# Where split weights stand in SBUF: from two pools on 512-byte boundaries to one ring whose blocks are offset for 256-column products

## The chip, the core and the metric

One core of one Trainium2 chip runs the whole kernel. The time is that of one execution on the device in microseconds, a median over runs. "The kernel before" is the version that the profile below was taken of, "after" the version with the change.

## What is computed

Two layers of an encoder trunk on 512 tokens of width 1024, in float32. Layer 0 mixes the tokens with retention and neighbourhood attention, layer 1 with a bidirectional SSD (Mamba-2) mixer. Each layer ends in the same channel mixer, which is where most of the changed products are:

```python
def conv_geglu_ffn(hn, w_up, conv_w, conv_b, w_down):
    u = depthwise_conv_centered(hn @ w_up, conv_w, conv_b)
    gate, val = jnp.split(u, 2, axis=-1)
    return (jax.nn.gelu(gate, approximate=True) * val) @ w_down

for layer in range(DEPTH):                      # DEPTH = 2
    hn = rms_norm(x, norm_mix_pre[layer])
    m = retention_na_mixer(hn, ...) if layer % 2 == 0 else ssd_mixer(hn, ...)
    x = x + rms_norm(m, norm_mix_post[layer])
    f = conv_geglu_ffn(rms_norm(x, norm_ffn_pre[layer]), ...)
    x = x + rms_norm(f, norm_ffn_post[layer])
```

w_up is 1024 x 5632 (22 tiles of 128 columns for the gate, 22 for the value), w_down 2816 x 1024.

## The kernel before

**Split operands.** TensorE multiplies in a float32 form of shorter mantissa (float32r). To keep float32 accuracy each operand is split into a high and a low part: ScalarE casts the source into the high part (L107), VectorE subtracts that from the source into the low part (L108). A product then takes three instructions, `mm3` (L114): high x high (L116), low x high (L117), high x low (L118). In projections to feature-major tiles the weights are the stationary operand, loaded into the array in blocks of 128 x 128 (128 partitions, 128 values of 4 bytes, so 512 bytes a partition), and the activations `xh`, `xl` stream through as 256 or 512 columns. In the profile PE is the stream of a product and PEld the load of its stationary block; the load of the next block runs while the present product streams.

**Weights on their way.** A weight unit is 128 x 1024 values. SyncE's queue loads it into one of three `wst` buffers; the split writes it into a buffer of the pool `whi` and one of `wlo`, four deep each (L41-42):

```python
hi, lo = self.whi.tile([P, 1024], R32, name="whi"), self.wlo.tile([P, 1024], R32, name="wlo")
with self.tc.high_priority(60):
    self.split(hi, lo, st, behind, low_behind)
```

This stands in `wunit` (L89), in `down_strassen` (L298), in `up_strassen` (L443) and, with 512 columns, in the step-size projection of the SSD mixer (L940). Each buffer starts on a multiple of 512 bytes, so every 128-column block does, too. In the step-size projection a block has only 64 columns, so every second one starts 256 bytes behind a boundary.

**Products with 256 columns.** Most products stream 512 columns. Three places stream 256:

- `up_strassen` (L429) computes two tiles each of gate and value as seven products of quarter matrices instead of eight. A call issues 7 x 2 x 4 `mm3`, 168 products, into `mm` and `pu` tiles. It is called at f = 6, 10, 14 and 18 (`UP`) of each FFN: eight calls. Its weights are sums of loaded units, made on VectorE ahead of the split. Its activations come from `combos` (L391), whose operands `xR`, `xS` go into tiles of the tags b1h, b1l, s3, e2.
- Each FFN starts with its first two tiles of gate and value in two halves of the tokens, since the second half is normalised later. The two units for the second tile are split into tiles that are free then, of the tags b1h, b1l and e2 (`extra`).
- The SSD mixer starts its first three tiles in halves likewise (L1224).

**The order of work.** A tile scheduler places the instructions of each engine by priorities from the order of the program; it may move those that aren't bound by data. Between engines semaphores hold the order. After the two halves the FFN goes tile by tile (f = 2 to 21), a tile being two units of 24 products of 512 columns, then a convolution on ScalarE (L507) and VectorE (L508, L509), gelu (L514) and the product of gate and value (L516). A down projection of seven quarter products with 512 columns (`down_strassen`) ends it. The SSD mixer (`mixer1`, L900) interleaves projections with the scan by hand-written lists of steps.

Of the kernel before, what the change touches and what calls it, by code (L numbers as in the profile page):

```python
# [8 lines left out]
F32 = mybir.dt.float32  # L9
R32 = mybir.dt.float32r  # L10
BF16 = mybir.dt.bfloat16
# [6 lines left out]
P = 128  # L18
S = 512
NT = S // P  # L20
D = 1024
# [4 lines left out]
HK = NF // 2  # L26
HW = S // 2
QUARTER = HK * P * S


class Env:


    def __init__(self, ctx, tc):
        self.tc, self.nc = tc, tc.nc
        nc = self.nc
        pool = lambda name, bufs, **kw: ctx.enter_context(tc.tile_pool(name=name, bufs=bufs, **kw))
        self.const = pool("const", 1)
        self.res = pool("res", 1)
        self.wst = pool("wst", 3)  # L40
        self.whi = pool("whi", 4)  # L41
        self.wlo = pool("wlo", 4)
        self.gain = pool("gain", 2)
        self.tmp = pool("tmp", 7)
        self.small = pool("small", 6)
        pool("pad", 1).tile([P, 48], F32, name="pad")
        self.mm = pool("mm", 4, space=PSUM)
        self.px = pool("px", 4, space=PSUM)
        self.dram = pool("dram", 1, space=DRAM)


        head = self.const.tile([P, 96 + P], F32, name="head")
        self.ident, self.mhalf = head[:, 96:], head[:, 0:1]
        make_identity(nc, self.ident)
        nc.vector.memset(self.mhalf, -0.5)

        xe = self.res.tile([P, NT, D + 32], F32, name="x")
        nc.vector.memset(xe[:, :, D:D + 1], (EPS * D) ** 0.5)
        self.x, self.xe = xe[:, :, :D], xe[:, :, :D + 1]
        self.junk = self.const.tile([P, 1280], BF16, name="junk")  # L60
        self.operands()
        self.late, self.xs, self.turned, self.chores = [], {}, {}, []

    def operands(self):
# [13 lines left out]
            self.together([m], [behind])  # L78
        return st

    def wunit(self, src, parts=None, st=None, behind=None, low_behind=None):

        if st is None:
            st = self.wload(src)
        halves = slice(0, 512), slice(512, 1024)
        if parts is None:
            hi, lo = self.whi.tile([P, 1024], R32, name="whi"), self.wlo.tile([P, 1024], R32, name="wlo")  # L89
            with self.tc.high_priority(60):  # L90
                self.split(hi, lo, st, behind, low_behind)
            return [(hi[:, c], lo[:, c]) for c in halves]
        with nullcontext() if behind else self.tc.high_priority(60):
            for j, c in enumerate(halves):
                self.split(parts[j], parts[j + 2], st[:, c], behind)
        return [(parts[j], parts[j + 2]) for j in range(2)]
# [181 lines left out]
def down_strassen(E, big, pool, w, ts, H, first, g_post, done):  # L278
# [15 lines left out]
    def weights(i, u, extra=None):  # L294
        cols = 1024 if u < HK // 2 else 512
        st = stage(i, u, cols)
        if extra is None:
            hi, lo = E.whi.tile([P, 1024], R32, name="whi"), E.wlo.tile([P, 1024], R32, name="wlo")  # L298
        else:
            hi, lo = extra[:, :1024], extra[:, 1024:]  # L300
        with tc.high_priority(150):
            E.split(hi[:, :cols], lo[:, :cols], st)
        return [(hi[:, c:c + 512], lo[:, c:c + 512]) for c in range(0, cols, 512)]
# [31 lines left out]
    st = {}  # L335
# [93 lines left out]
def up_strassen(E, w_up, f, X, G, V):  # L429
# [10 lines left out]
        return st  # L440

    def parts(st):
        hi, lo = E.whi.tile([P, 1024], R32, name="whi"), E.wlo.tile([P, 1024], R32, name="wlo")  # L443
        E.split(hi, lo, st)
        return hi, lo

# [49 lines left out]
def ffn(E, w_up, cw, w_down, ts, g_post_row, done, w1=None):  # L496
# [3 lines left out]
    with ExitStack() as ctx:  # L500
# [15 lines left out]
            nc.vector.tensor_tensor(H[:, f], g, v, op=ALU.mult)  # L516

        def extra(tags):
            t = [hp.tile([P, 2048 // len(tags)], R32, name="x" + n, tag=n) for n in tags]
            t = t if len(t) == 2 else [t[0][:, :1024], t[0][:, 1024:]]  # L520
            return [x[:, c:c + 512] for x in t for c in (0, 512)]

        u0, u1, st = w1 or (E.wunit(w_up[0, 0]), E.wunit(w_up[1, 0]), None)

        behind = E.turned[1][1] if w1 else None
        w0 = [[u0, u1], [E.wunit(w_up[0, 1], extra(("b1h", "b1l")), st, behind=behind),
                         E.wunit(w_up[1, 1], extra(("e2",)), behind=behind)]]
        cwt = cp.tile([P, 2, NF, 4], F32, name="cwt")
        nc.sync.dma_start(cwt, cw)
        cwn = cp.tile([P, NF, 3], F32, name="cwn")  # L530
# [369 lines left out]
def mixer1(E, w_dt, w_fm, cw, dtc, cols, mask, w_out, g_post_row, done, ahead):  # L900
# [8 lines left out]
    with ExitStack() as ctx:  # L909
# [1 line left out]
        one, two, four = pool("m1", 1), pool("m1b", 2), pool("m1d", 4)  # L911

        few = pool("m1s", 1)
        few.tile([P, 32], F32, name="gap")
        few.tile([P, 32], F32, name="pad")

        cwt = few.tile([P, NG, 6, 6], F32, name="cwt")
        nc.sync.dma_start(cwt, cw)
        um = one.tile([P, P], F32, name="um")
# [16 lines left out]
        def steps():  # L936

            st = E.wst.tile([P, 512], F32, name="wst")
            nc.sync.dma_start(st, w_dt)
            wh = E.whi.tile([P, 512], R32, name="whi")  # L940
            wl = E.wlo.tile([P, 512], R32, name="wlo")
            E.split(wh, wl, st)
            ps = E.mm.tile([P, S], F32, name="mm")
            for k in range(KD):
# [276 lines left out]
                project(o, i)  # L1221
            silus(o)

        w0 = [E.wunit(w_fm[0, i]) for i in range(3)]  # L1224
        p0 = [E.mm.tile([P, S], F32, name="mm") for _ in range(3)]
        for c in range(2):
            for i, (w, ps) in enumerate(zip(w0, p0)):
# [57 lines left out]
def trunk(tc, x, norms, ab, ssd, ffns, out):  # L1285

    nc = tc.nc
    with ExitStack() as ctx:
        E = Env(ctx, tc)
        w0 = []  # L1290
        for t in range(NT):
            nc.sync.dma_start(E.x[:, t, :], x[t * P:(t + 1) * P])
            if t == 0:
                g0 = E.bcast(norms[0, 0])

                nc.scalar.activation(E.junk[:, :1], E.mhalf, AF.Square)
            else:
                w0.append(E.wunit(ab[0][0, len(w0)]))
        for t in range(NT):
            E.norm(t, g0)  # L1300
            last = E.turn(t, 0 if t else 100)
            if t == 0:

                junk = E.px.tile([P, P], F32, name="idle", tag="px")
                E.together([nc.tensor.transpose(junk, E.ident, E.ident) for _ in range(6)], [last])

        def then(row):
            g = []

            def done(t):  # L1310
                if not g:
                    g.append(E.bcast(row))
                E.norm(t, g[0])
            return done

        def store(t):
            E.xs.pop(t, None)
            for h in range(2):
                c = slice(h * 512, h * 512 + 512)
                nc.sync.dma_start(out[t * P:(t + 1) * P, c], E.x[:, t, c])  # L1320

        ts = [E.dram.tile([4, QUARTER], F32, name=f"ts{i}") for i in range(2)]
        mixer0(E, w0, *ab, norms[0, 1], then(norms[0, 2]))
        E.chores = sums(E, ffns[0][2], ts[0])
        ffn(E, *ffns[0], ts[0], norms[0, 3], then(norms[1, 0]))
        w1 = []

        def ahead(w):
            up = ffns[1][0]
            w1.extend((E.wunit(up[0, 0]), E.wunit(up[1, 0], low_behind=w), E.wload(up[0, 1])))  # L1330

        mixer1(E, *ssd, norms[1, 1], then(norms[1, 2]), ahead)
        E.chores = sums(E, ffns[1][2], ts[1])
        ffn(E, *ffns[1], ts[1], norms[1, 3], store, w1)
        while E.late:
            E.flush()
# [119 lines left out]
```

## Time and profile before

| | us |
|---|---|
| median of three runs | 1370.33 (1370.28 to 1371.69) |
| the profiled execution | 1372.97 |
| its span, first to last instruction | 1371.2 |
| TensorE busy (PE) | 1344.3 |
| VectorE busy | 1088.5 |
| ScalarE busy | 815.2 |
| 24 products of 256 columns, by a stage's 20.15 for 168 | 2.88 |
| 24 products of 512 columns, by 80.00 for 353 | 5.44 |

A row of a group gives line, engine, operation, out <- in, count, busy time and the mean of one. A row of the timeline gives start and duration in us first. Products overlap: each lasts longer (0.28 us with 256 columns) than it is from its start to the next one's start (0.12 us), so the pace is read from starts or from counts in a stretch, not from durations. In the rows by stretches the columns are: the stretch, its length, then busy time and count of PE, PEld, VectorE, ScalarE and GpSimd, the granted share of the clock, the share of the DMA engines, and GB/s.

### The profile page before, as it was taken

The numbers are of one execution on the slowest core, as the hardware profiler recorded it, in microseconds if no ns is written. First come the engines' busy times: TensorE is split into PE (matmuls) and PEld (weight loads), VectorE is DVE, ScalarE is ACT, GpSimd is POOL, SyncE is SP. The second block draws the span as 40 slices with busy tenths as digits, with TensorE's granted clock in tenths as the row PEclk, the third lists the DMA queues.
The fourth block names the chain that finished last, engine by engine and source line by source line (L and its number), as shares of the span: only waits on it lengthen the run. The fifth ranks groups of instructions, "written<-read, shape, count | busy, mean of one in ns | idle before, by whom it ended". The sixth has DMA issues, their size and how long they took to land.

```text
span 1371.2 us, 19491 instructions
## 1 busy us (share of the span) xinstructions
PE 1344.3 (98%) x7352; PEld 1136.2 (83%) x7352; DVE 1088.5 (79%) x1524; ACT 815.2 (59%) x1345; POOL 111.5 (8%) x130
## 2 busy tenths in 40 slices
PE   7999999999999999999999999999999999999997
PEld 6877777798999888888778788787878899998886
DVE  7368878696768889697878876898789877888876
ACT  5356667453554566664878778477555455556563
POOL 1001110100111100020000110000010001110000
PEclk9999999999999999999999999999999999999999
DMA  7443232126779946654566455174433678994654
GB/s 298 144 138 99 89 100 93 49 93 218 256 210 233 250 147 193 197 201 128 142 180 194 119 178 179 48 204 110 147 128 127 224 249 214 234 242 131 196 179 145
DMA packets 73471, 229.90 MB, mean 168 GB/s; under 512 B 8352, under 2 KB 9120, under 8 KB 72864
## 3 DMA queue, kind: packets, MB, share of 16 engines
q1 hardware_dynamic: 58320, 167.30, 37.3%
q0 software_dynamic: 7168, 46.14, 13.4%
q10 hardware_dynamic: 7888, 15.21, 4.1%
q8 instruction: 58, 0.95, 0.3%
q14 instruction: 37, 0.30, 0.1%
HBM read 221.01 MB, written 51.64 MB: 199 GB/s over the span
## 4 chain that ended last, share of the span: by engine, by line
PE 83%; ACT 6%; DVE 5%; DMA 3%; issue 2%; POOL 1%; DVEq 0%; SPq 0%; POOLq 0%; ACTq 0%
PE mm L116 23%; PE mm L118 23%; PE mm L117 23%; PE pu L118 2%; PE pu L117 2%; PE pu L116 2%; PE pi L1122 1%; PE st L1071 1%; ACT pb L1101 1%; DMA pb<-pd 1%; PE py L1142 1%; ACT whi L107 1%; DVE wlo L108 1%; DMA wst<-in_c_fm 1%; PE pt L173 1%
## 5 line engine op out<-in xcount | busy, mean ns | idle before, releaser
L116 PE MATMUL mm<-xh,whi 128*128 128x512 f32 (+1 forms) x1024 | 382.5, 374 | 0.8 <-ACT z L1041 0.4
L118 PE MATMUL mm<-xl,whi 128*128 128x512 f32 (+1 forms) x1024 | 381.6, 373 | 1.0 <-DVE xl L108 0.5
L117 PE MATMUL mm<-xh,wlo 128*128 128x512 f32 (+1 forms) x1024 | 381.3, 373 | 1.0 <-DVE wlo L108 1.0
L108 DVE TENSOR_TENSOR wlo<-wst,whi 128x1024 fp32r<-128x1024 f32 (+1 forms) x232 | 280.9, 1216 | 89.9 <-ACT whi L107 88.3
L107 ACT CAST whi<-wst 128x1024 fp32r<-128x1024 f32 (+1 forms) x232 | 239.2, 1035 | 145.8 <-PE mm L117 63.5
L116 PEld LDWEIGHTS mm<-xh,whi 128*128 128x128 f32 x1024 | 192.6, 188 | 35.9 <-issue 2.3
L118 PEld LDWEIGHTS mm<-xl,whi 128*128 128x128 f32 x1024 | 192.2, 188 | 35.6 <-issue 1.3
L117 PEld LDWEIGHTS mm<-xh,wlo 128*128 128x128 f32 x1024 | 192.6, 188 | 34.2 <-DVE wlo L108 1.4
L1101 ACT ACTIVATE pb<-pb,tok 128x128 f32<-128x128 f32 x256 | 80.8, 393 | 9.3 <-DMA pb<-pd 7.9
L507 ACT ACTIVATE cv<-mm,cwt 128x512 f32<-128x512 f32 x56 | 43.5, 777 | 68.8 <-PE mm L118 68.7
L118 PE MATMUL mm<-wlo,ab1h 128*128 128x512 f32 x164 | 64.0, 390 | 0.4 <-DVE wlo L108 0.4
L116 PE MATMUL mm<-whi,ab1h 128*128 128x512 f32 x164 | 64.0, 390 | 0.0
L117 PE MATMUL mm<-whi,ab1l 128*128 128x512 f32 x164 | 63.8, 389 | 0.0
L508 DVE SCALAR_TENSOR_TENSOR cv<-mm,cwt,cv 128x511 f32<-128x511 f32 x56 | 41.7, 745 | 22.2 <-ACT cv L507 22.2
L514 ACT ACTIVATE cv<-cv 128x512 f32<-128x512 f32 x44 | 27.8, 632 | 42.8 <-DVE cv L509 42.8
L1035 DVE SCALAR_TENSOR_TENSOR xf<-mm,cwt,xf 128x511 f32<-128x511 f32 (+1 forms) x64 | 47.6, 745 | 6.2 <-ACT xf L1032 5.8
L274 POOL DMA_DIRECT2D ts<-in_f_down x48 | 30.0, 668 | 261.7 <-PE mm L118 227.7
L509 DVE SCALAR_TENSOR_TENSOR cv<-mm,cwt,cv 128x511 f32<-128x511 f32 x56 | 41.8, 746 | 0.9
L116 PE MATMUL mm<-whi,yh 128*128 128x512 f32 x104 | 40.8, 394 | 1.5 <-DVE xf L1035 1.5
L1154 POOL TENSOR_TENSOR sq<-sq 128x512 f32<-128x512 f32 x11 | 16.7, 1516 | 309.1 <-ACT sq L1148 244.6
L117 PE MATMUL mm<-whi,yl 128*128 128x512 f32 x104 | 41.1, 395 | 0.0
L116 PE MATMUL mm<-whi,xh 128*128 128x512 f32 x104 | 40.7, 398 | 0.0
(359 smaller groups left out, 2919.7 us busy)
## 6 DMA issues: line engine op xcount, KB each, us to landing
wst<-in_f_up SPq DMA_DIRECT2D x80, 512.0 KB
ts<-in_f_down POOLq DMA_DIRECT2D x48, 704.0 KB, 6.2
wst<-in_c_fm SPq DMA_DIRECT2D x40, 512.0 KB
wst<-ts SPq DMA_DIRECT2D x32, 512.0 KB
pb<-pd ACTq DMA_DIRECT2D x29, 512.0 KB
wst<-in_f_down SPq DMA_DIRECT2D x24, 512.0 KB
ts<-ts POOLq DMA_DIRECT2D x16, 704.0 KB, 9.9
wst<-in_ab_fm SPq DMA_DIRECT2D x20, 512.0 KB
```

The costliest lines, as they stand in the source:

```text
L107: first = self.nc.scalar.copy(hi, src)
L108: second = self.nc.vector.tensor_tensor(lo, src, hi.bitcast(F32), op=ALU.subtract)
L116: mm(out, lh, rh, start=first, stop=False)
L117: mm(out, ll, rh, start=False, stop=False)
L118: self.product = mm(out, lh, rl, start=False, stop=last)
L274: out.append(lambda i=i, src=src, j=j, c=c, kw=kw: gp.dma_start(part(ts, i, c), part(src, j, c), **kw))
L507: nc.scalar.activation(o, ps, AF.Identity, scale=w(1), bias=w(3))
L508: nc.vector.scalar_tensor_tensor(o[:, 1:], ps[:, :S - 1], w(0), o[:, 1:], op0=ALU.mult, op1=ALU.add)
L509: nc.vector.scalar_tensor_tensor(o[:, :S - 1], ps[:, 1:], w(2), o[:, :S - 1], op0=ALU.mult, op1=ALU.add)
L514: nc.scalar.activation(g, g, AF.Gelu_apprx_tanh)
L1035: nc.vector.scalar_tensor_tensor(r[:, a], ps[:, b], wc(j), r[:, a], op0=ALU.mult, op1=ALU.add)
L1101: nc.scalar.activation(pb[:, dr, c], pb[:, dr, c], AF.Identity, scale=1.0 - 2 * dr, bias=tok[:, 0, c, dr * H + h:dr * H + h + 1])
```

## The change

The pools `whi` and `wlo` go. One tile of the size [128, 4, 2048 + 128] takes their place, a ring of four slots that are used in turn; each holds a high and a low part with gaps around them. A new method gives a weight its two places:

```diff
+SKEW, GAP = 16, 128
...
+        self.ring = pool("ring", 1).tile([P, 4, 2048 + GAP], R32, name="ring")
+        self.turns = 0
...
-        self.whi = pool("whi", 4)
-        self.wlo = pool("wlo", 4)
...
-        self.small = pool("small", 6)
-        pool("pad", 1).tile([P, 48], F32, name="pad")
+        xe = pool("x", 1).tile([P, NT, D + 8], F32, name="x")
+        self.junk = pool("junk", 1).tile([P, 1056], BF16, name="junk")
+        self.small = pool("small", 4)
+        pool("pad", 1).tile([P, 16], F32, name="pad")
...
+    def weight(self, skew=0):
+
+        place = self.ring[:, self.turns % 4]
+        self.turns += 1
+        a, b = skew, 1024 + GAP - 3 * skew
+        return place[:, a:a + 1024], place[:, b:b + 1024]
...
     def parts(st):
-        hi, lo = E.whi.tile([P, 1024], R32, name="whi"), E.wlo.tile([P, 1024], R32, name="wlo")
+        hi, lo = E.weight(SKEW)
         E.split(hi, lo, st)
...
         def extra(tags):
-            t = [hp.tile([P, 2048 // len(tags)], R32, name="x" + n, tag=n) for n in tags]
+            t = [hp.tile([P, SKEW + 2048 // len(tags)], R32, name="x" + n, tag=n)[:, SKEW:] for n in tags]
...
-        u0, u1, st = w1 or (E.wunit(w_up[0, 0]), E.wunit(w_up[1, 0]), None)
+        u0, u1, st = w1 or (E.wunit(w_up[0, 0], skew=SKEW), E.wunit(w_up[1, 0], skew=SKEW), None)
...
-                         E.wunit(w_up[1, 1], extra(("e2",)), behind=behind)]]
+                         E.wunit(w_up[1, 1], extra(("s3",)), behind=behind)]]
...
-            wh = E.whi.tile([P, 512], R32, name="whi")
-            wl = E.wlo.tile([P, 512], R32, name="wlo")
+            wh, wl = (w[:, :512] for w in E.weight())
...
-        w0 = [E.wunit(w_fm[0, i]) for i in range(3)]
+        w0 = [E.wunit(w_fm[0, i], skew=SKEW) for i in range(3)]
```

With the skew of 16 values the high part starts 64 bytes behind a multiple of 512 bytes, the low part at (1152 - 48) x 4 = 4416, which is 320 behind one. Without it both start on a boundary. The weights of the three places with 256 columns get the skew, also those that the SSD mixer loads ahead for the second FFN; `wunit` without it, `down_strassen` and the step-size projection don't. In the FFN's `extra` tiles both parts start at 64. To make room, the rows of x lie 1032 instead of 1056 values apart, `junk` is shorter, `small` has four buffers of each tile instead of six, and two filler tiles in the SSD mixer are gone; the pools stand in another order. Apart from the skewed blocks, the operands of the split products start where they did within 512 bytes.

The instructions are the same, with other addresses. TensorE, SyncE and GpSimd have them in the same order, VectorE and ScalarE in a slightly other one. First place: VectorE at the start of the first FFN. `wlo_2936` and `wlo_2967` are the low parts of tile 3's two weights (gate, value), the `xS`, `xR` rows operands for the seven-product stages, the `cv` rows convolutions. Before:

```order
L108 TENSOR_TENSOR wlo_2936<-wst_2933,whi_2935 128x1024
L508 SCALAR_TENSOR_TENSOR cv1_2838<-mm_2610,cwt_2605,cv1_2838 128x511
L108 TENSOR_TENSOR xS2_3087<-H_2577,xS2_3087 128x1024
L509 SCALAR_TENSOR_TENSOR cv1_2838<-mm_2610,cwt_2605,cv1_2838 128x511
L108 TENSOR_TENSOR wlo_2967<-wst_2964,whi_2966 128x1024
L516 TENSOR_TENSOR H_2577<-cv0_2833,cv1_2838 128x512
L508 SCALAR_TENSOR_TENSOR cv0_2843<-mm_2611,cwt_2605,cv0_2843 128x511
```

And after, where the same two weights are read from `wst_2863` and `wst_2892`:

```order
L116 TENSOR_TENSOR ring_69<-wst_2863,ring_69 128x1024
L116 TENSOR_TENSOR xS4_3084<-H_2515,xS4_3084 128x1024
L516 SCALAR_TENSOR_TENSOR cv1_2772<-mm_2544,cwt_2539,cv1_2772 128x511
L516 SCALAR_TENSOR_TENSOR cv0_2777<-mm_2545,cwt_2539,cv0_2777 128x511
L517 SCALAR_TENSOR_TENSOR cv1_2772<-mm_2544,cwt_2539,cv1_2772 128x511
L517 SCALAR_TENSOR_TENSOR cv0_2777<-mm_2545,cwt_2539,cv0_2777 128x511
L524 TENSOR_TENSOR H_2515<-cv0_2767,cv1_2772 128x512
L516 SCALAR_TENSOR_TENSOR cv1_2782<-mm_2546,cwt_2539,cv1_2782 128x511
L116 TENSOR_TENSOR ring_69<-wst_2892,ring_69 128x1024
```

Between the two weights stood three instructions and stand seven now; `xS4`, whose tile e2 is free from the start now, takes the place of `xS2`, whose tile s3 holds a weight of the halves until they are done.

Second place: ScalarE in the SSD mixer, where it turns from exponentials (L1101, L1105) to the gates' silu (L1041, L1044) of the next group. Before:

```order
L1105 ACTIVATE e_6939<-pb_6532 128x512
L1041 ACT_TABLE_LOAD
L1041 ACTIVATE z_6751<-mm_6726 128x512
L1044 ACTIVATE bf_6501<-bf_6501 128x512
L1148 ACTIVATE sq_6763<-y_6570 128x512
L1162 ACTIVATE yh_6766<-y_6570,col_5699 128x512
L1044 ACTIVATE z_6617<-mm_6592 128x512
```

After:

```order
L1109 ACTIVATE e_6647<-pb_6256 128x512
L1105 ACTIVATE pb_6386<-pb_6386,tok_5456 128x128
L1045 ACT_TABLE_LOAD
L1045 ACTIVATE z_6467<-mm_6442 128x512
L1048 ACTIVATE bf_6225<-bf_6225 128x512
L1048 ACTIVATE z_6339<-mm_6314 128x512
L1152 ACTIVATE sq_6479<-y_6294 128x512
L1166 ACTIVATE yh_6482<-y_6294,col_5447 128x512
```

One exponential of the next head moves ahead of the change of tables, and one silu ahead of a square. There are 37 loads of tables on both sides.

More of the change, by code (lines that the diff above doesn't have):

```diff
@@ L39, in __init__ @@
         self.res = pool("res", 1)
+        self.operands()
+        self.tmp = pool("tmp", 7)
+        self.ring = pool("ring", 1).tile([P, 4, 2048 + GAP], R32, name="ring")
+        self.turns = 0
         self.wst = pool("wst", 3)
-        self.whi = pool("whi", 4)
-        self.wlo = pool("wlo", 4)
         self.gain = pool("gain", 2)
-        self.tmp = pool("tmp", 7)
-        self.small = pool("small", 6)
-        pool("pad", 1).tile([P, 48], F32, name="pad")
+        xe = pool("x", 1).tile([P, NT, D + 8], F32, name="x")
+        self.junk = pool("junk", 1).tile([P, 1056], BF16, name="junk")
+        self.small = pool("small", 4)
+        pool("pad", 1).tile([P, 16], F32, name="pad")
         self.mm = pool("mm", 4, space=PSUM)
@@ L55, in __init__ @@
         nc.vector.memset(self.mhalf, -0.5)
-        xe = self.res.tile([P, NT, D + 32], F32, name="x")
         nc.vector.memset(xe[:, :, D:D + 1], (EPS * D) ** 0.5)
         self.x, self.xe = xe[:, :, :D], xe[:, :, :D + 1]
-        self.junk = self.const.tile([P, 1280], BF16, name="junk")
-        self.operands()
         self.late, self.xs, self.turned, self.chores = [], {}, {}, []
@@ L79, in wload, with wunit @@
         return st
-    def wunit(self, src, parts=None, st=None, behind=None, low_behind=None):
+    def weight(self, skew=0):
[3 more added lines that the diff above has]
+        return place[:, a:a + 1024], place[:, b:b + 1024]
+    def wunit(self, src, parts=None, st=None, behind=None, low_behind=None, skew=0):
         if st is None:
@@ L88, in wunit @@
         if parts is None:
-            hi, lo = self.whi.tile([P, 1024], R32, name="whi"), self.wlo.tile([P, 1024], R32, name="wlo")
+            hi, lo = self.weight(skew)
             with self.tc.high_priority(60):
@@ L297, in weights @@
         if extra is None:
-            hi, lo = E.whi.tile([P, 1024], R32, name="whi"), E.wlo.tile([P, 1024], R32, name="wlo")
+            hi, lo = E.weight()
         else:
@@ L442, in parts @@
     def parts(st):
-        hi, lo = E.whi.tile([P, 1024], R32, name="whi"), E.wlo.tile([P, 1024], R32, name="wlo")
+        hi, lo = E.weight(SKEW)
         E.split(hi, lo, st)
@@ L913, in mixer1 @@
         few = pool("m1s", 1)
-        few.tile([P, 32], F32, name="gap")
-        few.tile([P, 32], F32, name="pad")
         cwt = few.tile([P, NG, 6, 6], F32, name="cwt")
@@ L1329, in ahead @@
             up = ffns[1][0]
-            w1.extend((E.wunit(up[0, 0]), E.wunit(up[1, 0], low_behind=w), E.wload(up[0, 1])))
+            w1.extend((E.wunit(up[0, 0], skew=SKEW), E.wunit(up[1, 0], low_behind=w, skew=SKEW), E.wload(up[0, 1])))
         mixer1(E, *ssd, norms[1, 1], then(norms[1, 2]), ahead)
```

## The prediction

> **What bounds the kernel now.** I read the page first: the busy rows, the clock, the chain.
>
> ```profile
> PE 1344.3 (98%) x7352; PEld 1136.2 (83%) x7352; DVE 1088.5 (79%) x1524; ACT 815.2 (59%) x1345; POOL 111.5 (8%) x130
> PEclk9999999999999999999999999999999999999999
> PE 83%; ACT 6%; DVE 5%; DMA 3%; issue 2%; POOL 1%; DVEq 0%; SPq 0%; POOLq 0%; ACTq 0%
> ```
>
> TensorE is busy for 98% of the span, its clock is granted throughout, and it carries 83% of the chain. So a shorter distance from one product to the next is a gain, as long as the weights arrive in time. What TensorE waits for (the view of waits, PE alone) is small; its longest row, and the only one that names a split weight's low part ahead of L117:
>
> ```profile
> PE pt L173 <- DVE xs L164: 9.8, 4, 7.5
> ...
> PE mm L117 <- DVE wlo L108: 1.0, 1, 1.0
> ```
>
> Next I cut the span into stretches that hold one kind of product. The first row below is the down projection of the first FFN (512 moving columns); the second is the 120 products with 256 columns after the transposes in that FFN's start; then come the eight seven-product stages (256 columns); the last is the SSD mixer. The count in the third column is of weight loads, one for each product.
>
> ```profile
> 510.00:590.00 80.00, 80.00 (x354) 66.28 (x353) 65.39 (x57) 50.97 (x57) 0.94 (x1) 1.00 0.56 180
> 284.69:299.15 14.46, 14.46 (x123) 14.46 (x121) 14.39 (x16) 8.23 (x11) 0.00 (x0) 1.00 0.12 36
> 342.70:362.85 20.15, 20.15 (x169) 20.14 (x168) 12.75 (x16) 11.75 (x19) 2.91 (x6) 1.00 0.69 243
> 384.64:404.79 20.15, 20.15 (x169) 20.14 (x168) 11.50 (x14) 9.54 (x16) 3.68 (x5) 1.00 0.77 206
> 426.58:446.73 20.15, 20.15 (x169) 20.15 (x168) 12.97 (x16) 11.10 (x17) 4.35 (x5) 1.00 0.94 213
> 468.52:488.67 20.15, 20.15 (x169) 20.15 (x168) 17.77 (x20) 13.80 (x21) 1.73 (x2) 1.00 0.89 246
> 1091.67:1111.82 20.15, 20.15 (x170) 20.15 (x168) 13.11 (x16) 12.09 (x19) 2.91 (x6) 1.00 0.71 242
> 1133.61:1153.76 20.15, 20.15 (x170) 20.15 (x168) 11.50 (x14) 9.45 (x15) 3.67 (x5) 1.00 0.78 205
> 1175.55:1195.70 20.15, 20.15 (x170) 20.15 (x168) 13.64 (x16) 11.65 (x19) 4.34 (x5) 1.00 0.96 218
> 1217.49:1237.64 20.15, 20.15 (x170) 20.15 (x168) 17.63 (x19) 13.80 (x21) 1.75 (x2) 1.00 0.82 215
> 627.00:1021.00 394.00, 388.79 (x2053) 313.57 (x2052) 315.78 (x482) 271.95 (x539) 24.46 (x19) 1.00 0.49 146
> ```
>
> A product with 512 columns comes every 80.00 / 353 = 0.2266 us, one with 256 columns every 20.15 / 168 = 0.1199 us, in all eight stages alike: TensorE waits for nothing there, yet half the columns cost more than half the time. Their difference, 0.1067 us, is what 256 columns stream in; so 0.1199 - 0.1067 = 13.2 ns of each product don't go with its width. That fixed part is what the change can touch.
>
> **The change part by part.** How many products: 8 stages x 168 = 1344 by the rows. At the start of each FFN two tiles times gate and value run in halves, 4 x 8 x 2 x 3 = 192 products, twice 384; the first three tiles of the SSD mixer 3 x 8 x 2 x 3 = 144. Together 1872. Before, every 128x128 block of their weights starts on a multiple of 512 bytes; after, the high part at 64 and the low part at 320 (in the FFNs' four extra units both at 64). The moving operands stay on the boundary, and the 512-column products keep boundary positions on both sides.
>
> What a different start is worth no row shows directly. Three rows come near. The entry to a stage:
>
> ```profile
> 342.48 0.39 PE L118 MATMUL mm<-xl,whi 128*128 128x512 f32 x1
> 342.70 0.28 PE L116 MATMUL mm<-xh,whi 128*128 128x256 f32 x1
> 342.81 0.28 PE L117 MATMUL mm<-xh,wlo 128*128 128x256 f32 x1
> 342.93 0.28 PE L118 MATMUL mm<-xl,whi 128*128 128x256 f32 x1
> ```
>
> The first two products with 256 columns are 0.11 us apart, the next 0.12, and then it stays: the same instructions with blocks on the same boundary can come faster, while the rhythm of load and stream isn't settled yet. So some of the 13 ns comes of how a load and a running product meet, not of the handover as such. Second, a row of the chain, where 128x128 loads follow each other with only 128 columns each:
>
> ```profile
> 722.37 1.34 PE pi L1122 x12
> ```
>
> 1.34 / 12 = 0.112 us, so a full load can follow a load 8 ns sooner than in the stages. Third, the only products of this kind whose blocks already stand off the boundary: the step-size projection (L940-944) has blocks of 64 columns, so every second one starts at 256 within 512.
>
> ```profile
> 638.55 0.39 PE L116 MATMUL mm<-xh,whi 128*64 128x512 f32 x1
> 638.78 0.40 PE L117 MATMUL mm<-xh,wlo 128*64 128x512 f32 x1
> 639.01 0.39 PE L118 MATMUL mm<-xl,whi 128*64 128x512 f32 x1
> 639.24 0.40 PE L116 MATMUL mm<-xh,whi 128*64 128x512 f32 x1
> 639.48 0.39 PE L117 MATMUL mm<-xh,wlo 128*64 128x512 f32 x1
> 639.71 0.39 PE L118 MATMUL mm<-xl,whi 128*64 128x512 f32 x1
> 639.93 0.39 PE L116 MATMUL mm<-xh,whi 128*64 128x512 f32 x1
> ```
>
> Six of them take 1.38 us, 0.230 each instead of 0.2266, and no longer evenly: 0.22 to 0.24. Their shape differs too, but they hint that the spacing is not indifferent to the position, and that it can also be worse.
>
> So the bounds per product are: all of the fixed part gone, 13.2 ns, 1872 x 13.2 = 24.7 us of gain; the spacing of L1122's row, 8 ns, 15.0 us; nothing, 0; and 3.4 ns more by the third case (230 less 226.6), 6.4 us lost. I take 0.115 us, the mean of the 0.11 and the 0.12 at the entry, which is the same product in the same place and so the nearest row: 5 ns x 1872 = 9.4 us.
>
> The Trainium skill, "TensorE: Matmul & The Clock Gate", section "Back-to-back issue gap", gives N / 2.4 + 2.5 ns for a lone product when warm, 109 ns for 256 columns; by that estimate the most to win would be 11 ns x 1872 = 20 us. The trace's 120 does not reach it.
>
> What must keep up when a stage shrinks to 168 x 0.115 = 19.3 us: VectorE has 17.77 us of work in the fullest stage (its row above), and the DMA engines 0.96 x 20.15 = 19.3 us in the third one. Both fit, the latter with nothing to spare; were the stage to go to 0.112, it would need 18.8 us, and DMA could hold back the two third stages (0.94 and 0.96) by about 0.5 us each. I count nothing for it in the forecast.
>
> Moved instructions. TensorE's, SyncE's and GpSimd's rows stand in the same order as before. On VectorE at the first FFN's start the low part of the second weight of tile 3 now stands behind four more instructions (the first place in the order shown above). What it had before:
>
> ```profile
> 298.69 1.21 DVE L108 TENSOR_TENSOR wlo<-wst,whi 128x1024 fp32r<-128x1024 f32 x1
> ```
>
> TensorE needs it after tile 2's two weights and tile 3's first, 72 products of 0.2266 from 299.15 on, so at 315.5 us: 15.6 us of cover after the split's end at 299.9, against four instructions of no more than the 1.21 us of this row. Cost nothing. In the SSD mixer ScalarE takes the same work in a slightly other order (second place shown above); TensorE idles 394.00 - 388.79 = 5.2 us in all there, so a change of order can give back little and cost little: 0, with ends of -1 and +2 us. The rows of x are 4128 bytes apart instead of 4224, and the small pool has 4 buffers instead of 6; no row shows a price; the nearest is the 9.8 us that the transposes wait in all (their row above), in which loads of x and the small tiles of the norms have a part, and I allow 0.5 us of it to either side and take 0. Whether high and low part share a ring slot or stand in two pools changes no release: a weight's two parts are turned over together on both sides, four deep.
>
> The profiled execution took 1372.97 us (span 1371.2), 2.64 over the median of 1370.33. 1372.97 - 9.4 = 1363.6 for it; against the median, 1370.33 - 9.4 = 1361.0 us.
>
> **The rivals.** *The position does nothing.* The fixed 13.2 ns would be the handover from product to product. For it: 512 columns, where a load has twice the time, carry the same remainder (0.2266 - 2 x 0.1067 = 13.2 ns). Against it: the 0.11 at the entry and the uneven third case. Then the time is 1370.3, give or take the 2 us of the moved instructions. The Trainium skill has the rule behind this: "TensorE: Matmul & The Clock Gate", section "Step-by-step: what each phase is for", says that the streaming operand and the weight load have SBUF read ports of their own and that loading the next weights takes nothing from the running product. By that rule no start address could matter; the trace's uneven rows speak mildly against it. Chance 0.17.
>
> *The load meets the stream worse.* The offset moves the point at which load and stream meet, and in the settled rhythm that may cost, as in the step-size rows. At 3.4 ns each, in all 1872 products, this gives 1370.3 + 6.4 = 1376.7; at 0.24 us for 0.2266, the worst gap there, it would be far more. It decides from 1.5 ns on (1872 x 1.5 = 2.8 us), a stage of 20.40 us instead of 20.15. Against it: the settled spacing on the boundary is already slower than the entry's. Chance 0.12.
>
> *All of it goes.* Spacing 0.109 to 0.112, the stages bounded by the stream alone: 1355 at 0.112, 1350 at 0.109. It shares the forecast's mechanism, and is in its chance.
>
> **How the numbers follow.** Some shortening by over 0.2% (2.7 us, about what a measurement of this kernel can tell from no change; its three runs lie 1.4 us apart) has 0.71, the position doing nothing 0.17, the worse meeting 0.12. The likeliest value is 1361. The range runs from 1350 (0.109 us a product) to 1372 (no effect, and the moved instructions cost 2 us): outside lie most of the worse meeting, 0.11, and a gain of over 20 us, 0.06.
>
> **What would show it.** Right: the eight stages shrink from 20.15 to about 19.3 us each with 168 loads, the start of each FFN by the same 5 ns a product, and 510 to 590 us keeps 353 loads in 80 us wherever that stretch then lies. No effect: the stages stay at 20.15. Worse: they grow beyond 20.40. Right for another reason: the stages stay and the SSD mixer's 5.2 us of idle time shrink. My step would be wrong in size if the stages go to 18.5 us or below, and wrong in kind if high and low parts behave differently (one of the three gaps in a triple shrinks, and the others don't).

## The result, and the profile after

The changed kernel takes 1367.76 us (median of 11 runs, 1365.52 to 1370.38) where the kernel before takes 1372.57 (11 runs beside it, 1370.28 to 1373.04). The ratio is 0.9971, with a 95% interval of 0.9961 to 0.9980: faster, by 4.0 us (0.29%). The forecast was a gain of 9.4 us. The profiled run of after took 1368.77 us, span 1367.0; before's span was 1371.2, so the profiled pair shows 4.2 us.

The page of after, busy row and shares of the chain:

```profile
PE 1341.5 (98%) x7352; PEld 1133.3 (83%) x7352; DVE 1087.6 (80%) x1524; ACT 813.5 (60%) x1345; POOL 112.6 (8%) x130
...
PE 83%; DVE 6%; ACT 4%; DMA 3%; issue 2%; POOL 1%; SPq 0%; DVEq 0%; POOLq 0%; ACTq 0%
```

The instructions are as many as before and TensorE still bounds the kernel. Its busy time shrank by 2.8 of the 4.2 us; as its products overlap in the profile, I don't lean on the split into busy and idle and go by stretches instead. Below: the start of the first FFN, the first and the last of the eight stages (the other six take 19.78 or 19.79 us), the down projection, the SSD mixer, and last 66 products with 256 columns inside that mixer.

```profile
285.24:299.45 14.21, 14.21 (x123) 14.21 (x122) 13.34 (x14) 6.81 (x9) 0.00 (x0) 1.00 0.11 31
343.00:362.79 19.79, 19.79 (x170) 19.79 (x169) 12.32 (x15) 11.44 (x18) 2.91 (x6) 1.00 0.72 244
...
1213.65:1233.44 19.79, 19.79 (x170) 19.79 (x168) 18.05 (x20) 13.72 (x22) 1.75 (x2) 1.00 0.88 235
510.00:590.00 80.00, 80.00 (x355) 66.24 (x354) 66.55 (x58) 51.10 (x59) 0.87 (x1) 1.00 0.56 182
624.40:1018.20 393.80, 388.84 (x2058) 313.68 (x2056) 316.51 (x485) 271.77 (x540) 24.45 (x19) 1.00 0.50 147
628.34:635.83 7.49, 7.49 (x67) 7.49 (x66) 4.15 (x7) 3.44 (x4) 0.00 (x0) 1.00 0.08 10
```

The same 66 products in the mixer of before:

```profile
630.20:638.10 7.90, 7.90 (x68) 7.90 (x66) 4.45 (x7) 3.43 (x4) 0.00 (x0) 1.00 0.09 16
```

Every stage goes from 20.15 to 19.79 us: 168 products at 117.8 ns each instead of 119.9. Eight times 0.36 is 2.9 us. The FFN's start shows the same 2.1 ns (14.46 to 14.21 for 120 products); over the 384 products of that kind that is, as an estimate, 0.8 us. The mixer's 66 products gain 0.41 us, of which the mixer as a whole keeps 0.2 (394.0 to 393.8); where the rest goes no run shows. Together 3.9 of the span's 4.2 us. The 512-column products keep their pace (354 loads in 80 us, 353 before).

Two paces are to be seen here, though. The 66 products of the mixer, with their blocks at the same places as those of the stages, come every 7.49 / 66 = 113.5 ns, against 119.7 before. And this is how a stage begins in after (the timeline of TensorE):

```profile
342.77 0.39 PE L126 MATMUL mm<-xl,ring 128*128 128x512 f32 x1
343.00 0.28 PE L124 MATMUL mm<-xh,ring 128*128 128x256 f32 x1
343.12 0.28 PE L125 MATMUL mm<-xh,ring 128*128 128x256 f32 x1
343.24 0.28 PE L126 MATMUL mm<-xl,ring 128*128 128x256 f32 x1
343.35 0.28 PE L124 MATMUL mm<-xh,ring 128*128 128x256 f32 x1
```

The first gap is 0.12 now (0.11 before the change), and the next ones stay there. So the change moved the settled pace of the stages by 2 ns, and somewhere else, at the same places, by 6.

Not all of the 0.41 us in the mixer is sure, though. Two of the runs below, pairs_one and pairs_three, leave these 66 products as they are in after, and there they take 7.77 us, 117.7 ns each. In pairs_one:

```profile
628.87:636.64 7.77, 7.77 (x67) 7.76 (x66) 4.37 (x7) 3.43 (x4) 0.00 (x0) 1.00 0.09 10
```

### The profile page after: what moved, and what is told of

The parts are those of the page before. It is cut to its first block, busy times and chain, and to the rows that moved or that the text cites. A ratio compares the mean times of both kernels' runs of the same rounds, so it can differ in the third digit from the quotient of the medians.

```text
span 1367.0 us, 19496 instructions
## 1 busy us (share of the span) xinstructions
PE 1341.5 (98%) x7352; PEld 1133.3 (83%) x7352; DVE 1087.6 (80%) x1524; ACT 813.5 (60%) x1345; POOL 112.6 (8%) x130
## 4 chain that ended last, share of the span: by engine, by line
PE 83%; DVE 6%; ACT 4%; DMA 3%; issue 2%; POOL 1%; SPq 0%; DVEq 0%; POOLq 0%; ACTq 0%
PE mm L124 23%; PE mm L126 23%; PE mm L125 23%; DMA pb<-pd 2%; PE pu L126 2%; PE pu L125 2%; PE pu L124 2%; PE pi L1126 1%; PE st L1075 1%; DVE ring L116 1%; PE py L1146 1%; DMA wst<-in_c_fm 1%; ACT pb L1105 1%; PE pt L181 1%; PE y L805 1%
## 5 line engine op out<-in xcount | busy, mean ns | idle before, releaser
L124 PE MATMUL mm<-xh,ring 128*128 128x512 f32 (+1 forms) x1024 | 382.0, 373 | 0.9 <-ACT z L1045 0.5
L126 PE MATMUL mm<-xl,ring 128*128 128x512 f32 (+1 forms) x1024 | 381.1, 373 | 1.0 <-DVE xl L116 0.5
L125 PE MATMUL mm<-xh,ring 128*128 128x512 f32 (+1 forms) x1024 | 380.8, 372 | 1.0 <-DVE ring L116 1.0
L116 DVE TENSOR_TENSOR ring<-wst,ring 128x1024 fp32r<-128x1024 f32 (+1 forms) x232 | 279.9, 1211 | 90.0 <-ACT ring L115 89.3
L115 ACT CAST ring<-wst 128x1024 fp32r<-128x1024 f32 (+1 forms) x232 | 239.0, 1034 | 150.1 <-PE mm L125 73.2
L124 PEld LDWEIGHTS mm<-xh,ring 128*128 128x128 f32 x1024 | 191.9, 187 | 36.3 <-issue 2.3
L126 PEld LDWEIGHTS mm<-xl,ring 128*128 128x128 f32 x1024 | 191.6, 187 | 35.5 <-issue 1.3
L125 PEld LDWEIGHTS mm<-xh,ring 128*128 128x128 f32 x1024 | 192.3, 188 | 34.3 <-DVE ring L116 1.4
L1105 ACT ACTIVATE pb<-pb,tok 128x128 f32<-128x128 f32 x256 | 80.8, 393 | 7.2 <-DMA pb<-pd 6.1
L124 PE MATMUL mm<-ring,ab1h 128*128 128x512 f32 x164 | 64.0, 390 | 0.0
L126 PE MATMUL mm<-ring,ab1h 128*128 128x512 f32 x164 | 63.9, 390 | 0.0
L125 PE MATMUL mm<-ring,ab1l 128*128 128x512 f32 x164 | 63.8, 389 | 0.0
L124 PE MATMUL mm<-ring,xh 128*128 128x512 f32 x104 | 41.3, 404 | 0.0
L125 PE MATMUL mm<-ring,yl 128*128 128x512 f32 x104 | 41.1, 395 | 0.0
```

Of the source, the lines that this page charges most:

```text
L115: first = self.nc.scalar.copy(hi, src)
L116: second = self.nc.vector.tensor_tensor(lo, src, hi.bitcast(F32), op=ALU.subtract)
L124: mm(out, lh, rh, start=first, stop=False)
L125: mm(out, ll, rh, start=False, stop=False)
L126: self.product = mm(out, lh, rl, start=False, stop=last)
L1105: nc.scalar.activation(pb[:, dr, c], pb[:, dr, c], AF.Identity, scale=1.0 - 2 * dr, bias=tok[:, 0, c, dr * H + h:dr * H + h + 1])
```

## The experiments

What had to be told apart: whether the gain is the offset at all, or the new pools and order; whether it is high part, low part, both, or their distance; why there are two paces; and whether the position that counts is that of the load alone or that of the load against the stream it meets. Since the eight stages took 20.15 us each to within 0.01, one kernel can carry eight variants, one for each stage, and its profile is the answer. "(64, 320)" below means: the blocks of the high part at 64 bytes within 512, those of the low part at 320.

**The layout without the offset.** All pools, sizes and orders of the change, but every block on the boundary:

```diff
-SKEW, GAP = 16, 128
+SKEW, GAP = 0, 128
```

> The changed kernel with a skew of 0: the ring, the other layout and the moved instructions stay, every block stands on the boundary. Theory P (position: the gain is the blocks' offset alone): the eight stages go back to 20.15 us, the time to that of the kernel before, a ratio of 0.999 to 1.001. Rival L (layout: x, the small pools or the moved instructions have a part in it): the stages are 20.15 us, but the ratio stays below 0.999.

Measured: 1373.01 us beside 1372.59, ratio 1.000 (0.9991 to 1.0009). Its first stage, in the view of stretches:

```profile
343.30:363.45 20.15, 20.15 (x170) 20.15 (x168) 13.12 (x16) 12.07 (x19) 2.90 (x6) 1.00 0.74 248
```

The stage is back at 20.15. To within the interval, 0.09%, all of the gain comes from the offset; the moved instructions, the small pools and the new row distances cost and bring nothing that can be measured.

**Eight pairs of places.** Each stage takes a pair of its own, in this order: (0, 0), (64, 320), (64, 64), (320, 320), (0, 64), (64, 0), (256, 256), (128, 384).

```diff
+PLACES = [(h // 4, l // 4) for h, l in ((0, 0), (64, 320), (64, 64), (320, 320), (0, 64), (64, 0), (256, 256), (128, 384))]
...
-        hi, lo = E.weight(SKEW)
+        hi, lo = E.weight(place)
...
+    place = PLACES.pop(0)
```

> Each of the eight stages has its own places of high and low part, in bytes behind a multiple of 512: (0,0), (64,320), (64,64), (320,320), (0,64), (64,0), (256,256), (128,384). Theory A (where load and stream meet within 512 bytes decides): (0,0) 20.15 us, (64,320) 19.79, the others differ from both and from each other, between 19.0 and 20.5. Theory B (only the boundary itself costs): every pair without a 0 takes 19.79 us, (64,0) 19.91 and (0,64) 20.03, as the low part is a third of the loads. If the low part's place has nothing to do with it, (64,64) and (64,0) take 19.79.

Measured (one run, 1369.97 us): the second to fourth stage took 19.79, 19.79 and 19.78 us. The rows of the first and of the last four:

```profile
343.04:363.19 20.15, 20.15 (x169) 20.15 (x168) 13.10 (x16) 12.09 (x19) 2.90 (x6) 1.00 0.71 241
...
1089.37:1109.15 19.78, 19.78 (x169) 19.77 (x168) 12.66 (x16) 11.73 (x19) 2.90 (x6) 1.00 0.72 243
1130.94:1150.73 19.79, 19.79 (x170) 19.79 (x168) 11.33 (x14) 9.44 (x16) 3.65 (x5) 1.00 0.79 205
1172.51:1192.66 20.15, 20.15 (x169) 20.14 (x168) 13.25 (x17) 11.26 (x18) 4.34 (x5) 1.00 0.97 220
1214.46:1234.63 20.17, 20.17 (x170) 20.17 (x168) 17.68 (x19) 13.81 (x21) 1.75 (x2) 1.00 0.82 210
```

The two rows below 20 us are the one-sided pairs (0, 64) and (64, 0): as good as both parts off, so the effect doesn't add up over the products of a triple. That goes against theory B, which had 20.03 and 19.91 for them. (256, 256) and (128, 384) are off the 512 boundary and gain nothing, so "off the boundary" isn't the rule. What helped in this run is 64 or 320, odd multiples of 64.

**Eight more pairs**, the same edit: (16, 16), (32, 32), (192, 192), (448, 448), (384, 128), (320, 64), (96, 352), (64, 192).

> As the run before with the places (16,16), (32,32), (192,192), (448,448), (384,128), (320,64), (96,352), (64,192). Theory A: several values, smooth or stepped in the offset, and (320,64) may differ from (64,320) by the order in which they follow. Theory B: all 19.79 us. Theory D (64 bytes is the grain): (16,16) and (32,32) like the boundary, 20.15 us, (96,352) like (64,320), 19.79.

Measured (one run, 1368.64 us): 19.88 for the first two, 19.79, 19.78 and 19.79 for (192, 192), (448, 448) and (320, 64), and then, with the fifth, the seventh and the eighth stage's rows:

```profile
1089.21:1109.38 20.17, 20.17 (x169) 20.16 (x168) 13.16 (x16) 12.23 (x21) 2.90 (x6) 1.00 0.75 255
...
1172.76:1192.47 19.71, 19.71 (x170) 19.71 (x168) 12.71 (x17) 10.75 (x17) 4.33 (x5) 1.00 0.96 218
1214.26:1233.31 19.05, 19.05 (x170) 19.05 (x168) 17.04 (x19) 13.06 (x19) 1.75 (x2) 1.00 0.86 226
```

(384, 128) is as bad as the boundary, and 16 and 32 are nearly as good as 64, so neither theory B nor theory D holds. (96, 352) is a little faster than 64. And one pair, (64, 192), falls out of the row: 19.05 us, 113.4 ns a product, the pace of the 66 products of the mixer.

**What comes ahead of a stage.** If there are two rhythms for the same addresses, what runs just ahead of a stage may pick one. So the places stay (64, 320), and ahead of stages 2 to 8 stand small products into an unused half of a bank (weight columns, moving columns, times): (64, 256, 1), (128, 128, 1), (128, 128, 2), (64, 64, 1), (64, 256, 2), (128, 64, 3), (64, 128, 4). They are added work and change no output.

```diff
+            E.nc.tensor.matmul(bank[0][:m, HW:HW + n], X["A11"][0][:, 0, :m], X["A11"][0][:, 1, :n], start=True, stop=True, skip_group_check=True)
...
+    kick(E, KICKS.pop(0), a, X)
```

> The changed kernel with a few extra small products ahead of each stage but the first, written beside the bank's used half: stationary columns, moving columns and number are none, (64,256,1), (128,128,1), (128,128,2), (64,64,1), (64,256,2), (128,64,3), (64,128,4). They leave no trace in the result. In the changed kernel 64 products in the SSD mixer run 113 ns apart and the stages 118 with blocks in the same places. Theory C (the products have two rhythms, and what comes ahead decides which): at least one of the stages runs at 113 to 114 ns, 19.0 to 19.2 us for 168 products. Theory A alone: all stages stay at 118 ns, 19.79 us and the extra products' 0.1 to 0.5 us.

Measured (one run, 1366.83 us), the first stage, which has none, and stages 3 to 6; stages 2, 7 and 8 took 19.79, 19.87 and 19.84:

```profile
341.19:360.98 19.79, 19.79 (x170) 19.79 (x168) 12.87 (x16) 11.96 (x19) 2.90 (x6) 1.00 0.74 248
...
424.52:444.36 19.84, 19.84 (x171) 19.84 (x169) 12.64 (x16) 10.74 (x17) 4.35 (x5) 1.00 0.96 214
466.31:485.43 19.12, 19.12 (x171) 19.12 (x170) 17.29 (x20) 13.49 (x21) 1.73 (x2) 1.00 0.94 256
1087.52:1106.65 19.13, 19.13 (x170) 19.13 (x169) 12.50 (x15) 11.61 (x19) 2.90 (x6) 1.00 0.72 250
1128.67:1147.73 19.06, 19.06 (x170) 19.06 (x169) 11.39 (x14) 9.42 (x15) 3.65 (x5) 1.00 0.79 206
```

Three of the seven additions take the whole stage of 168 products, about 0.7 us, from the slow rhythm into the fast one: 19.06 to 19.13 us. One product of 128x128 doesn't, two do. Each was run once. So there are two rhythms that keep themselves up, and the stage stays in the one that it falls into at its start. After's stages fall into the slow one; the mixer's 66 products fell into the fast one in after and into the slow one in pairs_one.

**The moving operand moved.** Position of the load in itself, or against the stream? The moving operands R1, S2 and S3 stand 64 bytes off, the other four on the boundary; the weights are at (0, 0) in the first FFN's stages, at (64, 64) in the second's.

```diff
-        x = pool.tile([P, 2, 4, HW], R32, name="x" + n, tag=tag)
+        m = 0 if tag == "e2" else 16
+        x = pool.tile([P, m + 8 * HW], R32, name="x" + n, tag=tag)[:, m:].rearrange("p (i k c) -> p i k c", i=2, k=4)
...
+PLACES = [(0, 0)] * 4 + [(16, 16)] * 4
```

> The changed kernel with the moving operands of three of the seven products (R1, S2, S3; 72 of a stage's 168 products) 64 bytes behind the boundary, the other four on it. The weights of the first FFN's stages are on the boundary, those of the second FFN's 64 bytes behind it. Theory R (only the distance between load and stream counts, modulo 128 bytes): in the first FFN the shifted products run at about 118 ns and the others at 120, a stage at 20.0 us; in the second FFN the shifted ones at 120, a stage at 19.9. Theory S (only the place of the load block counts): 20.15 us in the first FFN, 19.79 or, in the fast rhythm, 19.05 in the second.

Measured (one run, 1368.45 us). The parts A11, S3, S2 and A22 of the first FFN's first stage, 24 products each, then A11, S3, S2 and A22 of the second FFN's:

```profile
342.56:345.43 2.87, 2.87 (x26) 2.87 (x24) 1.83 (x3) 1.99 (x3) 0.97 (x2) 1.00 0.71 254
345.43:348.26 2.83, 2.83 (x27) 2.83 (x25) 2.63 (x3) 1.69 (x3) 0.00 (x0) 1.00 0.64 255
348.26:351.09 2.83, 2.83 (x27) 2.83 (x26) 1.23 (x1) 1.69 (x3) 0.00 (x0) 1.00 0.59 162
351.09:353.97 2.88, 2.88 (x27) 2.88 (x25) 1.33 (x2) 1.32 (x2) 0.96 (x2) 1.00 0.82 279
...
1089.15:1091.97 2.82, 2.82 (x25) 2.82 (x24) 1.77 (x3) 1.99 (x3) 0.97 (x2) 1.00 0.72 256
1091.97:1094.85 2.88, 2.88 (x26) 2.88 (x25) 2.69 (x3) 1.69 (x3) 0.00 (x0) 1.00 0.63 250
1094.85:1097.73 2.88, 2.88 (x26) 2.88 (x25) 1.22 (x1) 1.69 (x3) 0.00 (x0) 1.00 0.48 164
1097.73:1100.48 2.75, 2.75 (x26) 2.75 (x25) 1.19 (x2) 1.32 (x2) 0.96 (x2) 1.00 0.83 271
```

The tables mirror each other. With the weights on the boundary the two parts whose stream is off it are faster (2.83, 118 ns) and the others are as before (2.87 to 2.88). With the weights 64 bytes off, A11 on the boundary is fast (2.82), and S3 and S2, off by the same 64 as the weights, are back at 2.88 (120 ns), with no multiple of 512 anywhere on the weights' side. At the two distances tried, 0 and 64 bytes, what counts is the distance of load and stream and not the place of either. That is theory R, and the first FFN's stage takes its 20.00 us; the second FFN's takes 19.65 and not 19.9, since A22, which comes out of such a stretch, falls into the fast rhythm (2.75), and so do others behind it (the last part of that stage, S4, has 113.3 ns).

**The small products, with all blocks on the boundary.** The additions of the entry experiment together with `SKEW, GAP = 0, 128`.

> The extra small products ahead of the stages as in the run named entry, but all blocks on the boundary. Theory C1 (the offset is what lets the fast rhythm last): no stage leaves 120 ns, all 20.15 to 20.2 us. Theory C2 (the entry alone decides the rhythm): the stages after (128,128,2), (64,64,1) and (64,256,2) run at 113 to 114 ns, 19.05 to 19.15 us, here, too.

Measured (one run, 1373.33 us), stages 5 and 6, which with stage 4 (20.20 here) had the fast rhythm there:

```profile
1091.07:1111.30 20.23, 20.23 (x170) 20.23 (x169) 13.10 (x16) 12.07 (x19) 2.90 (x6) 1.00 0.73 251
1133.32:1153.47 20.15, 20.15 (x171) 20.15 (x169) 11.51 (x14) 9.49 (x16) 3.66 (x5) 1.00 0.77 204
```

None of the three leaves 20.15 by more than the additions themselves. With blocks and stream both on the boundary the entries that led into the fast rhythm don't lead there; it was seen only where there is an offset.

**Other places for the 512-column products.** Eleven up projection tiles of each FFN have their weights elsewhere:

```diff
-                w = E.wunit(None, st=st, behind=E.turned[3][1] if behind else None)
+                w = E.wunit(None, st=st, behind=E.turned[3][1] if behind else None, skew=WIDE.get(f, 0))
```

> The changed kernel in which the units of eleven tiles of each FFN with 512 columns stand at other places, bytes of high and low part: (0,0), (64,64), (64,192), (64,320), (192,192), (16,16), (32,32), (128,384), (256,256), (96,352), (0,64). Untouched, 512-column products run 226.6 ns apart. If a load that is off the boundary also spares a wide stream something (theory A): 224 to 226 ns at the odd multiples of 64, 226.6 at the multiples of 128. If the load has room enough beside a wide stream (theory E): 226.6 everywhere. If an offset disturbs the wide stream, as the step-size products with 0 and 256 in turn suggest: 228 to 231.

Measured (one run, 1370.18 us). Stretches of 24 products of the first FFN at (0, 0), (64, 64), (64, 320), (192, 192) and (256, 256):

```profile
308.80:314.24 5.44, 5.44 (x25) 4.50 (x24) 4.03 (x5) 2.00 (x3) 1.22 (x2) 1.00 0.97 345
319.68:325.28 5.60, 5.60 (x25) 4.51 (x24) 3.23 (x4) 1.71 (x2) 0.97 (x2) 1.00 0.90 327
366.66:372.25 5.59, 5.59 (x25) 4.51 (x24) 5.56 (x8) 2.49 (x4) 0.00 (x0) 1.00 0.56 178
372.25:377.74 5.49, 5.49 (x25) 4.51 (x24) 5.46 (x7) 1.83 (x2) 0.96 (x2) 1.00 0.76 282
455.62:461.07 5.45, 5.45 (x26) 4.50 (x24) 4.00 (x5) 1.83 (x2) 1.75 (x2) 1.00 1.07 354
```

Here the offset harms: 5.60 / 24 = 233 ns at (64, 64) against 227 at (0, 0) and (256, 256), with 229 at (192, 192). The rest lie between 231 and 234, so the theory that an offset disturbs the wide stream holds for all places tried here but (256, 256), with up to 3 ns more than it said. The offset of the change would have cost the 512-column products 6 ns each; that it is given to the 256-column ones alone matters.

The same run bears on the two rhythms. Its stages have the places of after, (64, 320), and no small products ahead, yet the first two of each FFN run in the fast rhythm and the last two in the slow one (19.79 us). The rows of the first two, then how the first begins:

```profile
342.01:361.06 19.05, 19.05 (x169) 19.05 (x168) 12.15 (x15) 11.28 (x18) 2.90 (x6) 1.00 0.74 250
383.24:402.29 19.05, 19.05 (x170) 19.04 (x168) 11.39 (x14) 9.45 (x15) 3.67 (x5) 1.00 0.80 205
...
342.01 0.28 PE L129 MATMUL mm<-xh,ring 128*128 128x256 f32 x1
342.13 0.28 PE L130 MATMUL mm<-xh,ring 128*128 128x256 f32 x1
342.25 0.28 PE L131 MATMUL mm<-xl,ring 128*128 128x256 f32 x1
```

The tiles ahead of them stand at (64, 192) and (192, 192), those ahead of the last two at (32, 32) and (256, 256). So the places of the wide products ahead of a stage can pick its rhythm, too. And a stage that runs at 113.4 ns begins with gaps of 0.12 us.

**The fast pair for all 1872 products.** (64, 192) instead of (64, 320), in the FFNs' extra units too:

```diff
-SKEW, GAP = 16, 128
+SKEW, GAP = (16, 48), 128
...
+            t = [hp.tile([P, SKEW[1] + 2048 // len(tags)], R32, name="x" + n, tag=n) for n in tags]
+            a, b = SKEW
+            t = [t[0][:, a:a + 1024], t[1][:, b:b + 1024]] if len(t) == 2 else [t[0][:, a:a + 1024], t[0][:, 1024 + b:]]
```

> The changed kernel with the places (64,192) instead of (64,320) for all 1872 products with 256 columns. Theory G (this pair of places leads into the fast rhythm by itself, as in the one stage that had it): all eight stages 19.05 us, 0.74 less than after the change, so about 8 x 0.74 = 5.9 us less than the changed kernel, 10 us or 0.7% less than before, a ratio of 0.993. Rival (that one stage came into the rhythm by chance): most stages stay at 19.79 us, the ratio at 0.997.

Measured: 1362.59 us (6 runs, 1360.77 to 1365.40) beside 1372.09, ratio 0.9932 (0.9917 to 0.9947). The first and the seventh stage:

```profile
340.79:359.83 19.04, 19.04 (x169) 19.04 (x168) 12.49 (x15) 11.60 (x19) 2.90 (x6) 1.00 0.76 251
...
1165.57:1184.61 19.04, 19.04 (x169) 19.04 (x168) 13.18 (x16) 10.22 (x17) 4.33 (x5) 1.00 1.00 232
```

All eight take 19.04 or 19.05 us, with no small products ahead of them. This kernel beats both: 9.3 us under before by the ratio (7.3 to 11.4), where after has 4.0. By the products it should be 6.5 ns x 1872 = 12.2 us, and the two profiled spans do lie 12.2 us apart (1371.2 and 1359.0); the median of its six runs shows less, and the interval ends at 11.4. The run with the profile was the shortest of the six, so the agreement of the spans is in part luck.

**Last pairs**, the edits of the pairs and of the wide places together. The stages: (192, 64), (64, 448), (320, 192), (192, 320), (0, 128), (64, 128), (192, 0), (0, 192).

> Two scans in one. The eight stages have (192,64), (64,448), (320,192), (192,320), (0,128), (64,128), (192,0), (0,192). Theory H (the fast rhythm needs high and low part at 64 and 192 modulo 256, in either order, so that the distance turns from load to load): the first four 19.05 us; the last four, with a part on a multiple of 128, 19.8 to 20.2. Rival (the order counts, low part above high part): (64,448) and (192,320) fast, (192,64) and (320,192) at 19.79. Rival (only the exact pair): none of them fast. And eleven tiles with 512 columns have (0,256), (256,0), (0,128), (192,448), (448,448), (224,224), (240,240), (480,480), (496,496), (128,0), (256,384): if a wide product has a fast place too, one of them shows under 226; if multiples of 256 are the best there is, (0,256) and (256,0) run at 226.6 and the others at 228 to 235.

Measured (one run, 1370.95 us), the first three stages, then 24 products with 512 columns each at (448, 448), (240, 240) and (496, 496):

```profile
341.69:361.66 19.97, 19.97 (x169) 19.97 (x168) 12.55 (x16) 11.66 (x19) 2.90 (x6) 1.00 0.77 259
383.63:402.69 19.06, 19.06 (x170) 19.05 (x169) 11.39 (x14) 9.45 (x15) 3.67 (x5) 1.00 0.80 206
424.78:443.83 19.05, 19.05 (x169) 19.05 (x168) 13.12 (x17) 9.56 (x16) 4.34 (x5) 1.00 0.94 208
...
372.65:378.14 5.49, 5.49 (x25) 4.51 (x24) 5.46 (x7) 1.83 (x2) 0.96 (x2) 1.00 0.74 263
419.34:424.78 5.44, 5.44 (x25) 4.50 (x24) 5.41 (x7) 2.37 (x3) 0.00 (x0) 1.00 1.05 239
460.49:465.93 5.44, 5.44 (x26) 4.50 (x24) 5.40 (x7) 2.53 (x4) 0.00 (x0) 1.00 1.07 216
```

The others took 19.97, 20.00, 19.86, 19.79 and 19.79. None of the three expectations for the stages holds as it stands. High part at 64 and low part at 192 modulo 256 came with the fast rhythm in all three such pairs tried; the two swapped gives 19.97, slower than (64, 64). That the pair alone does it is shown for (64, 192), in fast_all. Here the wide tiles ahead of the stages stood at other places, too: ahead of (64, 448) a tile at (448, 448), and wide_places has shown that a tile ahead can pick the rhythm. So the rule modulo 256 is likely and not shown. Of the 512-column products none came faster than 226.7 ns. (0, 256) and (256, 0) have that pace, as was expected of the multiples of 256, but so do (240, 240) and (496, 496), which was not.

## Why the prediction was right and wrong

**What bounds the kernel: right.** The gain is in the spacing of the 256-column products and, as far as layout_only can tell (ratio 1.000 without the offset), nowhere else. Their stretches, with the one estimate above, add up to 3.9 of 4.2 us.

**The fixed part: right that it could shrink, wrong in what it was.** The prediction held that 13.2 ns of each product don't go with its width. At the best places seen, 256 columns take 113.4 ns and 512 take 226.7, twice as much. By these two paces nothing fixed is left: 6.6 of the 13.2 ns hung on the places, and the other 6.6 go with the width. No run came near the bound of 24.7 us, nor to the 109 to 112 ns of "all of it goes". That 512 columns leave the same remainder was no evidence for the first rival, either: the 0.1067 us had been worked out as the difference of the two paces, so the two remainders are equal by construction.

**The term that was off: "I take 0.115 us, the mean of the 0.11 and the 0.12 at the entry".** It measured 0.1178 in the stages, 2.15 ns a product instead of 5; times 1872 that is 4.0 us instead of 9.4. The mechanism was the forecast one, and this term was mis-sized. It failed because the gap at an entry doesn't tell the settled pace. On the boundary the first gap is 0.11 us and the stage settles at 120 ns; in after it is 0.12 and the stage settles at 117.8; in wide_places it is 0.12, too, and the stage settles at 113.4. Nor is there a pace halfway: a stage at (64, 320) has either of two rhythms, 117.8 or 113.4 ns. At the one pace throughout the gain would be 4 us, at the other 12, and no row of before shows either. After's stages took the first, fast_all's the second.

**The idea that load and running product meet: right as far as the runs go.** The prediction said that some of the 13 ns comes of how a load and a running product meet. The mirrored tables of moving_offset show that the distance of the two addresses counts. Why it does is not shown by any run. The row from which the idea was drawn, the shorter gap at the entry, does not bear it out, as said above; that the offset came out on the faster side owes something to luck. The sign for "wrong in kind" didn't come: by the starts in the trace the three gaps of a triple average 117.7, 118.3 and 117.3 ns in after's first stage, so all three shrank.

**The rival "the position does nothing" falls**, with 20.15 against 19.79 for the same kernel with and without the offset. The Trainium skill, "TensorE: Matmul & The Clock Gate", section "Step-by-step: what each phase is for", from which this rival could be had, says that stream and weight load read through ports of their own; the runs disagree with the conclusion that addresses can't matter: 113.4 to 120.1 ns by place alone. The Trainium skill, same page, section "Back-to-back issue gap", gives 109 ns for a lone product of 256 columns; by that estimate the stages would take 18.3 us. None came under 19.04.

**The rival "the load meets the stream worse" falls for 256 columns**: the worst places had 20.17 us, 0.02 over the boundary. It would have held for 512 columns (233 ns against 227), and the change leaves those alone.

**The third nearest row misled in part.** From the step-size products (0.22 to 0.24, blocks at 0 and 256 in turn) I took a bound of 3.4 ns lost. 512-column products at (256, 256), and in the last run at (0, 256) and (256, 0), come every 226.7 ns as on the boundary, so their unevenness isn't the position 256 in full blocks. Whether it is their 64 columns was not tried.

**The terms set to nothing: right.** The second weight of tile 3, the order on ScalarE, the pitch of x and the small pool together cost under the 0.09% of layout_only's interval. The longest waits of TensorE stand as they stood (the view of waits of after):

```profile
PE pt L181 <- DVE xs L172: 9.7, 4, 7.3
...
PE mm L125 <- DVE ring L116: 1.0, 1, 1.0
```

**What must keep up: right, and with more room than I gave it.** I held it possible that DMA would hold back the third stages by 0.5 us at 0.112 us a product. At 0.1134 it has a share of 1.00 there, and the stage takes 19.04 like the others.

## What to carry to other kernels

Where TensorE runs back to back, read the pace of each kind of product from the loads in a stretch, and don't take the first gaps for a sign of the settled pace. In this kernel, split weights for 256 moving columns belong at 64 (high) and 192 (low) with the stream on the boundary, and those for 512 columns at multiples of 256. Stages that repeat make a cheap bench: give each its own variant, and one profile compares eight.

## What the runs showed of the hardware

- For 128x128 weights against 256 moving columns (4 bytes an element, stream on a multiple of 512 bytes), the spacing depends on where the weights stand, (high, low) in bytes within 512: 120.0 ns at (0, 0), (256, 256), (128, 384) and (384, 128), 119.0 at (0, 128), 118.9 at (192, 64) and (192, 320), 118.3 at (16, 16) and (32, 32), 118.2 at (64, 128), 117.8 at (64, 64), (192, 192), (320, 320), (448, 448), (64, 320) and (320, 64), 117.3 at (96, 352), 113.4 at (64, 192).
- With weights and stream both 64 bytes off it is 120 again, with the stream alone off 118 (moving_offset).
- One part off the boundary does as much as both: (0, 64), (64, 0), (192, 0) and (0, 192) have 117.8 as well.
- With the same instructions and places (64, 320) there are two rhythms, 117.8 and about 113.4 ns. Each lasts for a whole stage. One or two small products ahead of the stage can decide which it is, and so can the places of the wide products ahead; with all on the boundary the same small products led to no fast stage.
- For 512 columns the order is another: 226.7 ns at multiples of 256 and at 240 and 496, 229 at 192 and 448, 231 to 234 at the other places tried. Why the two kinds differ, and why high and low can't be swapped, stays open.
